# The down projection of a feed-forward layer by quarters, with seven products in place of eight

## The chip, the cores and the metric

The kernel runs on one core of one Trainium2 chip. The metric is the device time of one launch in microseconds (us). The engines are TensorE (PE, with its weight loads as PEld), VectorE (DVE), ScalarE (ACT), GpSimd (POOL) and SyncE (SP), which here only issues DMA transfers. Each engine works through its own instructions in the order in which they were written; semaphores between the engines are set by what reads and writes each buffer.

## The reference

Two transformer blocks on 512 tokens of width 1024, in float32. What the change touches is the end of the second block: a gated feed-forward layer with 2816 inner columns, whose last product is the down projection, and the final norm.

```python
h = rmsnorm_2(x, ffn_norm_g[l])
x = x + (jax.nn.silu(h @ w_gate[l]) * (h @ w_up[l])) @ w_down[l]
...
return rmsnorm_2(x, final_norm_g)
```

Here `w_down` is 2816 x 1024, so the last product is (512 x 2816) @ (2816 x 1024).

## The kernel before

Every float32 product is made of three fast ones: each operand is split into a rounded high part and the rest, and high x high, high x low and low x high are summed in PSUM. An activation block of 128 x 128 is loaded into TensorE as the stationary side, and 512 columns of weights stream past it.

**Weights.** All weights come as one stream of chunks, each 128 x 1024 elements (512 KB: two blocks of 128 rows by 512 columns). For a chunk, SP issues the load into `raw`, a ring of two buffers (`load_to`, L265); ACT copies it to `wh`, the high part (L290); DVE subtracts to get `wl` (L291), which is the last reader of the raw buffer, so that the chunk after the next may be loaded into it. `wh` and `wl` have four buffers each. When TensorE has used chunk i for the last time, `used(i)` calls for the conversion of chunks up to i + 3 and the loading of those up to i + 5. The position of these calls in the program sets the order on SP, ACT and DVE.

**Gate and up.** The two products ahead of the last one are already made with seven products of quarters (class `Sevenfold`): the weights' quarters are loaded (class `Quarters`, tiles `quart`), and DVE adds and subtracts them (L203, tiles `qsum`). The result, the gated activations, stands in three tiles `fa`.

**Down projection.** `dn0` and `dn1` are the two halves of 512 output columns. Each has 22 blocks of 128 inner rows (11 chunks), and every chunk is used by 2 row blocks x 4 token blocks x 3 = 24 matmuls of 512 columns (L378); the two products have 2 x 22 x 4 x 3 = 528 of them. `place` splits the activations from `fa` into `fs` (ACT L480, DVE L481). `ev_dn` adds a finished block to `x5` (DVE L1455), sums the squares (ACT L501), and in the second half makes the norm's factor on POOL (`rstd2`, L493 to L496), scales (ACT L1462, DVE L1463) and sends the block to DRAM.

**Elsewhere.** In the first block's attention POOL normalises the probabilities P (L568, L569), which TensorE then transposes (L607); in the norms POOL makes `var` and `rstd`.

Of the kernel before, what the change touches and what calls it, by code (L numbers as in the profile page):

```python
# [11 lines left out]
F32 = mybir.dt.float32  # L12
FR = mybir.dt.float32r
# [4 lines left out]
S = 512  # L18
# [10 lines left out]
def two_blocks_kernel(  # L29
# [143 lines left out]
    class Quarters:  # L173

        n_loads, n_sums = 0, 0

        def __init__(self, w, c0, n):
            self.w, self.c0, self.half, self.parts = w, c0, n // 2, {}

# [3 lines left out]
        def load(self, name):  # L183
            i, Quarters.n_loads = Quarters.n_loads % 6, Quarters.n_loads + 1
            if i not in ring:
                if i < 4:
                    if 0 not in ring:
                        t = unit("quart", "U3", [128, 4, 1024], F32)
                        ring.update({j: t[:, j, :] for j in range(4)})
                else:  # L190
                    ring[i] = pool.tile([128, 1024], F32, name="quart", tag="raw", bufs=2)
            t = self.parts[name] = self.view(ring[i])
            c, k = self.c0 + self.half * (name[1] == "2"), 512 * (name[2] == "2")
            nc.sync.dma_start(t, self.w[k:k + 512, c:c + self.half].rearrange("(k p) c -> p k c", p=128))
# [19 lines left out]

    specs["fg0"] = ([(w_gate_2, 0, 512, 0)], 8)
    specs_tail = {f"dn{i}": ([(w_down_2, 512 * i, 512, 0)], 22) for i in range(2)}
    quartered = []
    for i in range(6):
        for w in (w_gate_2, w_up_2):
            quartered.append(Quarters(w, 512 * i, 512 if i < 5 else 256))  # L220

# [27 lines left out]
    def load_to(i):  # L249
        while len(raws) <= min(i, len(stream) - 1):  # L250
# [11 lines left out]
            for w, c0, n, at, *heads in pieces:  # L262
                src = w[k0 * 128:(k0 + nk) * 128, c0:c0 + (heads[1] * heads[2] if heads else n)]
                if not heads:
                    nc.sync.dma_start(raw[:, :, at:at + n], src.rearrange("(k p) c -> p k c", p=128))  # L265
                    continue
# [7 lines left out]
    def convert_to(i):  # L274
        while len(ws) <= min(i, len(stream) - 1):
# [13 lines left out]
            for js in [slice(j, min(nk, j + cut)) for j in range(0, nk, cut)]:  # L289
                nc.scalar.copy(hi[:, js], raw[:, js])  # L290
# [13 lines left out]
    side = []  # L304
    mark = [None]
    last_plain = [None]
# [191 lines left out]

    def sum_sq(src, ss, n=512):
        j = p2("junk")  # L500
        nc.scalar.activation(j[:, :n], src, AF.Square, accum_out=ss)  # L501
# [813 lines left out]

    def fa_at(c):
        i = c // 8
        if i not in fa_tiles:
            fa_tiles[i] = unit("fa", ("U5", "U2", "U4")[i], dt=F32)
        return fa_tiles[i], c % 8  # L1320

    class Sevenfold:
# [14 lines left out]
        def out(self, half, t, v):  # L1337

            c, n = half * self.n, self.n
            tok = slice(256 * t, 256 * t + 256)  # L1340
# [7 lines left out]
            else:  # L1348
                ft, at = fa_at(4 * (self.g // 2) + c)
                nc.vector.tensor_mul(ft[:, at:at + n, tok], v, gates[half][:, :n, tok])  # L1350
# [80 lines left out]
    fparts = []  # L1431

    def place(i):
        while len(fparts) <= min(21, i + 3):
            j = len(fparts)
            if j < 20:
                if j % 4 == 0:
                    t = unit("fs", ("U0", "U6", "U1", "U5", "U2")[j // 4])
                    fparts_at[0] = t
                hi, lo = fparts_at[0][:, j % 4, :], fparts_at[0][:, 4 + j % 4, :]  # L1440
            else:
                t = pool.tile([128, 2, 512], FR, name="fs", tag=f"V{j - 20}")
                hi, lo = t[:, 0, :], t[:, 1, :]
            ft, at = fa_at(j)
            split(hi, lo, ft[:, at, :], 0.5)
            fparts.append((hi, lo))
        return fparts[i]

    fparts_at = [None]

    def ev_dn(nh):
        def f(tb, ps):
            c = halves[nh]
            xx = x5[:, tb, c]
            nc.vector.tensor_add(xx, xx, ps)  # L1455
            sum_sq(xx, ssf[:, tb, nh:nh + 1])
            if nh == 0:
                nc.gpsimd.tensor_mul(xx, xx, gfin[:, c])  # L1458
                return
            r = rstd2(ssf[:, tb, :], D)  # L1460
            xa = x5[:, tb, halves[0]]
            nc.scalar.activation(xa, xa, AF.Copy, scale=r)  # L1462
            nc.vector.scalar_tensor_tensor(xx, xx, r, gfin[:, c], op0=OP.mult, op1=OP.mult)  # L1463
            for q in halves if tb == NB - 1 else [slice(0, 1024)]:
                nc.sync.dma_start(ov[:, tb, q], x5[:, tb, q])
        return f

    for nh in range(2):
        run(product(f"dn{nh}", place, ev_dn(nh), True, "mid" if nh == 0 else "tail"))

# [48 lines left out]
```

## Time and profile before

| what | value |
|---|---|
| time, median of 3 runs | 1212.84 us (1212.43 to 1214.42) |
| the profiled execution: its time, its span | 1213.95 us, 1212.2 us |
| PE busy in the span | 1180.9 us (97%) |
| DVE, ACT, POOL busy | 798.0 us (66%), 611.9 us (50%), 234.8 us (19%) |
| share of the 16 DMA engines in use, rate | 30.7%, 97 GB/s |
| the chain that ended last: share of PE | 85% |

The span is the time from the first to the last instruction that the profiler recorded; the launch's own time has 1.75 us around it. The times of the runs are without the profiler. The rows of a trace carry the line of the kernel (L378) and the names of the tiles, output first: `mm<-wh,fs` writes `mm` from `wh` and `fs`. Matmuls are pipelined, so a row's length reaches into the next row: the distance between starts is the cost.

### The profile page before, as it was taken

The page shows a single profiled execution, that of the slowest core. Times are in us where ns is not written, and L with a number is a line of the kernel's source. Part 1 is how long each engine was busy: PE and PEld are TensorE (multiplying, and loading weights), DVE is VectorE, ACT ScalarE, POOL GpSimd, SP SyncE. Part 2 cuts the span into 40 slices and gives each one's busy share as a digit, 9 for nine tenths or more (in the row PEclk, how much of TensorE's full clock was granted, in tenths as well). Part 3 has the DMA queues.
Part 4 walks back from the last instruction along what each step waited for, and adds up shares of the span by engine and source line. Part 5 has one row for each costly group of instructions (what it writes and reads, how often), then busy time and mean ns, then how long its engine had stood idle before and what let it go on. Part 6 is the DMA issues. An engine that isn't in the chain of part 4 may idle for free.

```text
span 1212.2 us, 18380 instructions
## 1 busy us (share of the span) xinstructions
PE 1180.9 (97%) x6700; PEld 1020.6 (84%) x6700; DVE 798.0 (66%) x1526; ACT 611.9 (50%) x1239; POOL 234.8 (19%) x468
## 2 busy tenths in 40 slices
PE   6999999999999999999999999999999999999997
PEld 5898888888888888789888788788899999988885
DVE  5578767796575744785555578773898888793322
ACT  4466456535663444534566667632655544472212
POOL 2011065403341020301433435400000000000201
PEclk9999999999999999999999999999999999999999
DMA  5422302221222532334222221353333342243221
GB/s 192 99 69 70 122 19 70 83 90 44 70 87 88 191 112 92 127 91 115 55 85 83 52 64 53 115 180 107 122 105 119 91 122 79 62 174 122 87 87 70
DMA packets 81946, 117.16 MB, mean 97 GB/s; under 512 B 14528, under 2 KB 44480, under 8 KB 81856
## 3 DMA queue, kind: packets, MB, share of 16 engines
q1 hardware_dynamic: 81856, 115.99, 30.7%
q8 instruction: 53, 0.87, 0.3%
q14 instruction: 37, 0.30, 0.1%
HBM read 109.68 MB, written 6.29 MB: 96 GB/s over the span
## 4 chain that ended last, share of the span: by engine, by line
PE 85%; DVE 5%; issue 3%; ACT 2%; DMA 2%; POOL 1%; SPq 0%; POOLq 0%; DVEq 0%; ACTq 0%
PE mm L378 58%; PE mm L1360 7%; PE R L1360 5%; PE E L1360 5%; PE AV L622 3%; PE T L607 2%; DVE wl L291 2%; DMA raw<-in_w_in_dram 1%; PE T L509 1%; PE S L841 1%; PE S L840 1%; DMA raw<-in_w_branch_b_dram 1%; ACT wh L290 0%; POOL rstd L487 0%; PE S L1189 0%
## 5 line engine op out<-in xcount | busy, mean ns | idle before, releaser
L291 DVE TENSOR_TENSOR wl<-raw,wh 128x512 fp32r<-128x512 f32 (+4 forms) x199 | 183.0, 938 | 146.4 <-ACT wh L290 145.3
L290 ACT CAST wh<-raw 128x512 fp32r<-128x512 f32 (+4 forms) x199 | 155.7, 806 | 195.1 <-PE mm L378 127.0
L378 PE MATMUL mm<-wh,fs 128*128 128x512 f32 x352 | 110.6, 395 | 1.6 <-ACT fs L480 1.6
L568 POOL TENSOR_TENSOR rr<-rs,mone 128x1 f32<-128x1 f32 x128 | 76.4, 597 | 167.4 <-ACT P L562 107.4
L378 PE MATMUL mm<-hh,wh 128*128 128x512 f32 x256 | 103.6, 405 | 0.0
L478 DVE TENSOR_TENSOR pl<-T,ph 128x128 fp32r<-128x128 f32 (+3 forms) x152 | 62.0, 412 | 60.5 <-ACT ph L477 60.0
L378 PE MATMUL mm<-hl,wh 128*128 128x512 f32 x256 | 101.4, 396 | 0.0
L378 PE MATMUL mm<-hh,wl 128*128 128x512 f32 x256 | 100.5, 395 | 0.0
L378 PEld LDWEIGHTS mm<-wh,fs 128*128 128x128 f32 x352 | 65.9, 188 | 18.0 <-ACT fs L480 1.8
L562 ACT ACTIVATE P<-P,nm 128x128 f32<-128x128 f32 (+2 forms) x96 | 51.5, 536 | 51.2 <-DVE nm L555 47.7
L477 ACT CAST ph<-T 128x128 fp32r<-128x128 f32 (+3 forms) x152 | 54.7, 362 | 42.6 <-PE T L607 31.4
L569 POOL TENSOR_SCALAR P<-P,rr 128x256 f32<-128x256 f32 (+3 forms) x128 | 71.8, 561 | 12.0
L290 ACT CAST wh<-qsum 128x1024 fp32r<-128x1024 f32 (+1 forms) x44 | 42.7, 974 | 54.6 <-PE R L1360 23.2
L378 PE MATMUL mm<-wl,fs 128*128 128x512 f32 x176 | 69.7, 397 | 0.3 <-DVE wl L291 0.3
L1458 POOL TENSOR_TENSOR x<-x,gb 128x512 f32<-128x512 f32 x4 | 6.1, 1542 | 283.7 <-ACT junk L501 283.7
L291 DVE TENSOR_TENSOR wl<-qsum,wh 128x1024 fp32r<-128x1024 f32 (+1 forms) x44 | 49.5, 1126 | 13.4 <-ACT wh L290 13.4
L607 PE MATMUL T<-ident,P 128*128 128x128 f32 x296 | 54.6, 278 | 3.7 <-ACT km L1140 2.8
L1360 PE MATMUL R<-acts,wh 128*128 128x256 f32 x320 | 57.8, 281 | 0.0
L1360 PE MATMUL mm<-acts,wh 128*128 128x256 f32 x320 | 57.6, 281 | 0.0
L378 PEld LDWEIGHTS mm<-hh,wl 128*128 128x128 f32 x256 | 48.1, 188 | 11.2
L1360 PE MATMUL E<-acts,wh 128*128 128x256 f32 x320 | 57.1, 281 | 0.0
L378 PEld LDWEIGHTS mm<-hh,wh 128*128 128x128 f32 x256 | 48.2, 188 | 8.6
(410 smaller groups left out, 3338.2 us busy)
## 6 DMA issues: line engine op xcount, KB each, us to landing
raw<-in_w_in_dram SPq DMA_DIRECT2D x50, 512.0 KB, 3.7
raw<-in_w_down_dram SPq DMA_DIRECT2D x22, 512.0 KB, 3.7
quart<-in_w_up_dram SPq DMA_DIRECT2D x20, 512.0 KB, 4.0
raw<-in_w_merge_dram SPq DMA_DIRECT2D x16, 512.0 KB, 3.6
raw<-in_w_out_dram SPq DMA_DIRECT2D x16, 512.0 KB, 4.0
quart<-in_w_gate_dram SPq DMA_DIRECT2D x16, 512.0 KB, 3.9
raw<-in_w_ple_gate_dram SPq DMA_DIRECT2D x8, 512.0 KB, 4.1
raw<-in_w_branch_b_dram SPq DMA_DIRECT2D x4, 512.0 KB, 3.5
```

The costliest lines, as they stand in the source:

```text
L290: nc.scalar.copy(hi[:, js], raw[:, js])
L291: mark[0] = nc.vector.tensor_sub(lo[:, js], raw[:, js], hi[:, js].bitcast(F32)).ins
L378: nc.tensor.matmul(o, x_, m, start=kc == 0 and k == 0 and n0 == 0, stop=last and k == 2)
L477: nc.scalar.copy(hi, src)
L478: nc.vector.tensor_sub(lo, src, hi.bitcast(F32))
L509: nc.tensor.transpose(T[:, i, :], src[:, blk(c + i)], ident)
L562: nc.scalar.activation(P[:, :n], P[:, :n], AF.Exp, bias=bias, scale=-1.0, accum_out=rs)
L568: nc.gpsimd.tensor_tensor(rr, rs, mone, op=OP.pow)
L569: nc.gpsimd.tensor_scalar(P[:, :n], P[:, :n], rr, 1.0, op0=OP.mult, op1=OP.mult)
L607: nc.tensor.transpose(T[:, i, :], P[:, blk(i)], ident)
L622: nc.tensor.matmul(self.av[:, q0:q0 + pc.stop - pc.start], self.v(kb), m, start=pi == 0 and i == 0, stop=pi == len(plan) - 1 and i == 1)
L1360: nc.tensor.matmul(R[:, c, :], w[:, kc, cs], m[:, kc, :], start=first and c + kc + k == 0, stop=kc == 3 and k == 2, skip_group_check=True)
```

## The change

The down projection is made with seven products on quarters in place of eight (`DOWN`). Both operands are cut in two by two: inner rows by 1408, output columns by 512, tokens by 256. Each product has 11 blocks of 128 inner rows and 2 token blocks, so 66 matmuls; seven have 462. The four weight operands that are sums of quarters, S1 to S4, are made in DRAM: 16 transfers of 352 x 512 elements (704 KB) copy quarters into `down_sums` (on SP's queue, behind the loads of chunks 14, 16, ... 44), and 16 transfers of the same size, issued by POOL, add other quarters to them (at chunks 46, 48, ... 76; each behind a one-column copy `poke` from that chunk's `wh`, which fixes its place). The products S1 to S4 then load their chunks from there. A product of 11 blocks has five full chunks and one of half the size, so 42 chunks in place of 22, and a chunk serves 12 matmuls in place of 24.

The activations' sums T1 to T4 are made by DVE in place on `fa` (L1494) and split (ACT L518, DVE L519) in three parts while the product ahead runs. Results that are not accumulated in PSUM are added to `x5` by DVE (L1517). `x5` now comes in eight loads of 256 KB (L1476) in place of four of 512 KB. For the pairing of columns in `fa`, gate and up take their quarters from columns c and c + 1408, and the chunk `fg0` comes in two loads of 256 columns.

```diff
-    specs["fg0"] = ([(w_gate_2, 0, 512, 0)], 8)
-    specs_tail = {f"dn{i}": ([(w_down_2, 512 * i, 512, 0)], 22) for i in range(2)}
+    specs["fg0"] = ([(w_gate_2, 0, 256, 0), (w_gate_2, DFF // 2, 256, 256)], 8)
+    down_sums = {f"S{i}": tc.dram_tile([DFF // 2, 512], F32, name=f"down{i}") for i in range(1, 5)}
+    DOWN = ("A11", "S4", "A12", "S1", "S2", "S3", "A22")
+    specs_tail = {f"dn{name}": ([(down(name), 0, 512, 0)], 11) for name in DOWN}
+    behind, poke = {}, pool.tile([128, 1], F32, name="poke", tag="poke")
+    def plan_sums():
+        copies = [("S1", "A21"), ("S3", "A11"), ("S2", "A11"), ("S4", "A12")]
+        adds = [("S1", "A22"), ("S3", "A21"), ("S2", "S1"), ("S4", "S2")]
+        at = 14
+        for some, engine in ((copies, nc.sync), (adds, nc.gpsimd)):
+            for dst, src in some:
+                for r in range(0, DFF // 2, 352):
+                    behind[at] = (engine, down_sums[dst][r:r + 352, :], down(src)[r:r + 352, :])
+                    at += 2
+    def send(i, hi):
...
+        if engine is nc.sync:
+            with tc.issue_after(loads[0]):
+                engine.dma_start(dst, src)
+        else:
+            with tc.issue_after(engine.tensor_copy(poke, hi[:, 0, 0:1].bitcast(F32)).ins):
+                engine.dma_start(dst, src, accum_op=OP.add, max_dma_last_dim=512)
...
+            send(len(ws), hi)
             ws.append((hi, lo))
...
-    x5 = unit("x5", "U3", [128, NB, 1024], F32)
-    for tb in range(NB):
-        nc.sync.dma_start(x5[:, tb, :], x4v[:, tb, :])
...
-    for nh in range(2):
-        run(product(f"dn{nh}", place, ev_dn(nh), True, "mid" if nh == 0 else "tail"))
+        for b in range(2):
+            nc.sync.dma_start(x5[i, t][b], x4v[:, 2 * t + b, halves[i]])
...
+    def fs_make(name, part):
+        if name in T_OF:
+            d, a, op, b = T_OF[name]
+            nc.vector.tensor_tensor(fa(d, part), fa(a, part), fa(b, part), op=op)
+            src = fa(d, part)
...
+        split(hi, lo, src, 0.5)
...
+    def add_to(i, t, R, op=OP.add):
+        for b in range(2):
+            xx = x5[i, t][b]
+            nc.vector.tensor_tensor(xx, xx, R[b], op=op)
...
+        elif name == "S2":
+            add_to(0, 1, R["U"], OP.subtract)
+            first_done(0, 1)
+            add_to(1, 1, R["U"])
+            add_to(1, 0, R["U"])
...
+        for i, (kc, b) in enumerate(seq):
+            if n < 6 and i in (2, 8, 14):
+                with tc.issue_after(mark[0]), tc.issue_after(mark_hi[0]):
+                    fs_make(DN_ACT[DOWN[n + 1]], i // 6)
+            if n < 4 and i == 10:
+                x_load(*((0, 1), (0, 0), (1, 1), (1, 0))[n])
+            g, j = divmod(kc, 2)
+            convert_to(f0 + g)
...
+            for k, (a, w) in enumerate(((ah, wh), (ah, wl), (al, wh))):
+                nc.tensor.matmul(acc[b], a, w[:, j], start=first and kc == 0 and k == 0, stop=kc == 10 and k == 2,
+                                 skip_group_check=True)
+            if end_of[g] == i:
+                used(f0 + g)
```

Three places of the written order show where instructions now stand. The first is DVE in the down projection, before: the end of the first half `dn0`, with its four additions to `x5`, between the conversions of the chunks.

```order
L291 TENSOR_TENSOR wl_11880<-raw_11814,wh_11879 128x1024
L291 TENSOR_TENSOR wl_11913<-raw_11848,wh_11912 128x1024
L1455 TENSOR_TENSOR x5_11558<-x5_11558,mm_11563 128x512
L1455 TENSOR_TENSOR x5_11558<-x5_11558,mm_11582 128x512
L1455 TENSOR_TENSOR x5_11558<-x5_11558,mm_11589 128x512
L1455 TENSOR_TENSOR x5_11558<-x5_11558,mm_11596 128x512
L291 TENSOR_TENSOR wl_11955<-raw_11883,wh_11954 128x1024
```

DVE after, from the first chunk of product S3 (`wl_12166`) to its third (`wl_12205`); L328 is the same subtraction as L291 above.

```order
L328 TENSOR_TENSOR wl_12166<-raw_12130,wh_12165 128x1024
L1494 TENSOR_TENSOR fa_11214<-fa_11214 128x3x256
L1517 TENSOR_TENSOR x5_11675<-x5_11675,mm_11741 128x512
L1517 TENSOR_TENSOR x5_11910<-x5_11910,mm_11741 128x512
L1517 TENSOR_TENSOR x5_12038<-x5_12038,mm_11741 128x512
L1517 TENSOR_TENSOR x5_11675<-x5_11675,mm_11742 128x512
L1517 TENSOR_TENSOR x5_11911<-x5_11911,mm_11742 128x512
L1517 TENSOR_TENSOR x5_12039<-x5_12039,mm_11742 128x512
L519 SCALAR_TENSOR_TENSOR fs_12117<-fa_10305,fs_12117 128x1024
L328 TENSOR_TENSOR wl_12187<-raw_12148,wh_12186 128x1024
L519 SCALAR_TENSOR_TENSOR fs_12061<-fa_11214,fs_12061 128x768
L328 TENSOR_TENSOR wl_12205<-raw_12169,wh_12204 128x1024
```

Between two subtractions that free the same raw buffer there now stand the last part of the sum, six additions, two splits and the other buffer's subtraction; before, at most four additions and one subtraction.

The second place is SP at the start of the down projection, before.

```order
L265 DMA raw_11449<-in_w_down_2_dram 128x2x512
L265 DMA raw_11470<-in_w_down_2_dram 128x2x512
L103 DMA gb_11556<-in_final_norm_g_2_dram 128x1024
L1429 DMA x5_11558<-x4d_8583 128x1024 x4
L265 DMA raw_11489<-in_w_down_2_dram 128x2x512
L265 DMA raw_11512<-in_w_down_2_dram 128x2x512
L265 DMA raw_11531<-in_w_down_2_dram 128x2x512
```

SP after, the same place.

```order
L302 DMA raw_11506<-in_w_down_2_dram 128x2x512
L302 DMA raw_11527<-in_w_down_2_dram 128x2x512
L103 DMA gb_11613<-in_final_norm_g_2_dram 128x1024
L302 DMA raw_11546<-in_w_down_2_dram 128x2x512
L1476 DMA x5_11675<-x4d_8636 128x512
L302 DMA raw_11569<-in_w_down_2_dram 128x2x512
L1476 DMA x5_11675<-x4d_8636 128x512
L1476 DMA x5_11794<-x4d_8636 128x512 x2
L1476 DMA x5_11910<-x4d_8636 128x512
L1476 DMA x5_11911<-x4d_8636 128x512
L1476 DMA x5_12038<-x4d_8636 128x512
L1476 DMA x5_12039<-x4d_8636 128x512
L302 DMA raw_11588<-in_w_down_2_dram 128x2x512
```

All eight loads of `x5` now stand ahead of the load of the first product's fifth chunk.

The third place is POOL in the norm that begins the second block, before.

```order
L493 TENSOR_SCALAR var<-ssg 128x1
L494 TENSOR_SCALAR var<-ssg,var 128x1
L496 TENSOR_TENSOR rstd<-var,mhalf 128x1
L485 TENSOR_SCALAR var<-ss 128x1
L487 TENSOR_TENSOR rstd<-var,mhalf 128x1
```

POOL after, the same place (the lines of the norm are now L523 to L534).

```order
L531 TENSOR_SCALAR var<-ssg 128x1
L249 COPY poke<-wh 128x1
L250 DMA down_82<-down_80 1408x128
L532 TENSOR_SCALAR var<-ssg,var 128x1
L534 TENSOR_TENSOR rstd<-var,mhalf 128x1
L523 TENSOR_SCALAR var<-ss 128x1
L525 TENSOR_TENSOR rstd<-var,mhalf 128x1
```

An addition for S4 (`down_82`), in 1408 pieces of 128 elements, now stands between the two steps of `var`. The other twelve additions stand in the same way between the POOL instructions of the attention (S1) and of what follows it (S3, S2).

## Rows read from the trace of the kernel before

**Rows 1.** Page: busy time, share of the span, instructions of each engine

```profile
PE 1180.9 (97%) x6700; PEld 1020.6 (84%) x6700; DVE 798.0 (66%) x1526; ACT 611.9 (50%) x1239; POOL 234.8 (19%) x468
```

**Rows 2.** Busy time by stretch: last product, and what follows it

```profile
core 0: us, PE busy (x) PEld busy (x) DVE busy (x) ACT busy (x) POOL busy (x), PEclk, DMA share, GB/s
1077.00:1204.60 127.60, 126.68 (x552) 101.70 (x552) 46.63 (x56) 38.02 (x57) 9.74 (x14) 1.00 0.29 97
1204.60:1212.20 7.60, 0.00 (x0) 0.00 (x0) 1.96 (x3) 2.02 (x4) 1.47 (x3) 0.70 0.46 180
```

**Rows 3.** Groups of instructions by line, 1077 to 1213 us

```profile
L378 PE MATMUL mm<-wh,fs 128*128 128x512 f32 x352 | 110.6, 395 | 1.6 <-ACT fs L480 1.6
L291 DVE TENSOR_TENSOR wl<-raw,wh 128x1024 fp32r<-128x1024 f32 x22 | 28.0, 1273 | 63.0 <-ACT wh L290 63.0
L290 ACT CAST wh<-raw 128x1024 fp32r<-128x1024 f32 x21 | 22.0, 1049 | 67.1 <-PE mm L378 57.2 <-DMA raw<-in_w_down_dram 5.3 <-issue 4.6
L501 ACT ACTIVATE junk<-x 128x512 f32<-128x512 f32 x8 | 5.0, 627 | 17.5 <-DVE x L1455 17.5
L1462 ACT ACTIVATE x<-x,rstd 128x512 f32<-128x512 f32 x4 | 2.9, 724 | 4.4 <-POOL rstd L496 4.4
```

**Rows 4.** Timeline of PE: start, length, instruction, idle time ahead

```profile
1077.57 0.72 PE L378 MATMUL mm<-wh,fs 128*128 128x512 f32 x2 [1.58 <-ACT fs L480]
...
1179.70 0.62 PE L378 MATMUL mm<-wh,fs 128*128 128x512 f32 x2
...
1181.10 0.62 PE L378 MATMUL mm<-wh,fs 128*128 128x512 f32 x2
```

**Rows 5.** DMA issues from 1060 us: count, size, median us to landing

```profile
raw<-in_w_down_dram SPq DMA_DIRECT2D x22, 512.0 KB, 3.7
x<-x4d SPq DMA_DIRECT2D x4, 512.0 KB, 5.5
```

**Rows 6.** Timelines of SP, ACT, DVE: one raw buffer's turn

```profile
1095.65 0.37 SPq L265 DMA_DIRECT2D raw<-in_w_down_dram  x1
...
1099.48 1.05 ACT L290 CAST wh<-raw 128x1024 fp32r<-128x1024 f32 x1 [3.82 <-DMA raw<-in_w_down_dram]
...
1100.56 1.23 DVE L291 TENSOR_TENSOR wl<-raw,wh 128x1024 fp32r<-128x1024 f32 x1 [3.64 <-ACT wh L290]
...
1101.82 0.37 SPq L265 DMA_DIRECT2D raw<-in_w_down_dram  x1
```

**Rows 7.** Timeline of DVE: instructions directly behind one another

```profile
866.12 0.69 DVE L478 TENSOR_TENSOR acts<-h3f,acts 128x512 fp32r<-128x512 f32 x1
866.72 1.22 DVE L203 TENSOR_TENSOR qsum<-qsum,quart 128x1024 f32<-128x1024 f32 x1
867.85 1.22 DVE L203 TENSOR_TENSOR qsum<-quart 128x1024 f32<-128x1024 f32 x1
```

**Rows 8.** Timeline of SP: the issue of two loads

```profile
1066.88 0.88 SPq L265 DMA_DIRECT2D raw<-in_w_down_dram  x2
```

**Rows 9.** Timelines of POOL and PE: a probability block and its transpose

```profile
336.19 0.79 POOL L569 TENSOR_SCALAR P<-P,rr 128x128 f32<-128x128 f32 x1
...
340.27 0.27 PE L607 MATMUL T<-ident,P 128*128 128x128 f32 x1
```

**Rows 10.** Busy time by stretch: where S3's sums are issued

```profile
400.00:420.00 20.00, 20.00 (x92) 16.26 (x91) 12.88 (x19) 6.90 (x12) 0.00 (x0) 1.00 0.70 237
```

**Rows 11.** Timeline of POOL in the norm at 500 us

```profile
503.73 0.86 POOL L494 TENSOR_SCALAR var<-ssg,var 128x1 f32<-128x1 f32 x1 [3.44 <-ACT junk L501]
```

**Rows 12.** Timeline of PE: a pause and the clock behind it

```profile
696.20 0.69 PE L607 MATMUL T<-ident,P 128*128 128x128 f32 x2 [2.79 <-ACT km L1140]
...
697.12 0.63 PE L378 MATMUL mm<-ckl,wh 128*128 128x512 f32 x1
...
699.18 0.40 PE L378 MATMUL mm<-wh,cq 128*128 128x512 f32 x1
```

More of the change, by code (lines that the diff above doesn't have):

```diff
@@ L264, in load_to @@
                 if not heads:
-                    nc.sync.dma_start(raw[:, :, at:at + n], src.rearrange("(k p) c -> p k c", p=128))
+                    loads[0] = nc.sync.dma_start(raw[:, :, at:at + n], src.rearrange("(k p) c -> p k c", p=128)).ins
                     continue
@@ L1314, in two_blocks_kernel, with fa_at @@
     fa_tiles, gates = {}, {}
[L1316 to L1320, printed above, removed]
+    def fa_at(i, half):
+        if i // 2 not in fa_tiles:
+            fa_tiles[i // 2] = unit("fa", ("U5", "U2", "U4")[i // 2], dt=F32)
+        return fa_tiles[i // 2], 4 * half + 2 * (i % 2)
     class Sevenfold:
@@ L1449, in two_blocks_kernel @@
[L1449 to L1466, printed above, removed]
@@ L1468, in two_blocks_kernel, with x_load, fa @@
-    for nh in range(2):
-        run(product(f"dn{nh}", place, ev_dn(nh), True, "mid" if nh == 0 else "tail"))
+    x5 = {}
+    def x_load(i, t):
+        if i == 0:
+            q = pool.tile([128, 2, 512], F32, name="x5", tag=f"V{t}")
+            x5[i, t] = [q[:, 0, :], q[:, 1, :]]
+        else:
+            x5[i, t] = [p2("x5") for _ in range(2)]
+        for b in range(2):
+            nc.sync.dma_start(x5[i, t][b], x4v[:, 2 * t + b, halves[i]])
+    def fa(name, part):
+        f, t = int(name[1]) - 1, int(name[2]) - 1
+        n = 4 if part < 2 else 3
+        return fa_tiles[part][:, 4 * f:4 * f + n, 256 * t:256 * t + 256]
@@ new lines, in two_blocks_kernel, with dn_banks, dn_end @@
+    R = {}
+    def dn_banks(kinds):
+        return [{"mm": mm_bank, "S": s_bank, "AV": av_bank,
+                 "T": lambda: t_bank("E").rearrange("p a b -> p (a b)")}[k]() for k in kinds]
+    def dn_end(name):
+        if name == "A11":
+            R["U"] = dn_banks(("mm", "mm"))
+            for b in range(2):
+                nc.scalar.activation(R["U"][b], R["A11"][b], AF.Copy, scale=-1.0)
+        elif name == "S4":
+            add_to(0, 1, R["S4"])
+        elif name == "A12":
+            add_to(0, 0, R["A11"])
+            first_done(0, 0)
+        elif name == "S1":
+            add_to(0, 1, R["S1"])
+            add_to(1, 1, R["S1"], OP.subtract)
+        elif name == "S2":
[3 more added lines that the diff above has]
+            add_to(1, 0, R["U"])
+        elif name == "S3":
+            add_to(1, 1, R["S3"])
+            for b in range(2):
+                last_done(b, 1)
+            add_to(1, 0, R["S3"])
@@ new lines, in two_blocks_kernel, with dn_product @@
+    DN_ACT = {"A11": "B11", "S4": "B22", "A12": "B21", "S1": "T1", "S2": "T2", "S3": "T3", "A22": "T4"}
+    DN_BANK = {"A11": ("S", "S"), "S4": ("T", "T"), "S1": ("mm", "AV"), "S3": ("T", "T"), "A22": ("S", "S")}
+    def dn_product(n, name):
+        into = {"A12": "A11", "S2": "U"}.get(name, name)
+        if into not in R:
+            R[into] = dn_banks(DN_BANK[name])
+        acc, f0, first = R[into], first_of[f"dn{name}"], into == name
+        seq = [(kc, b) for kc in range(11) for b in range(2)]
+        if n == 6:
+            seq = seq[:16] + [(kc, b) for b in range(2) for kc in range(8, 11)]
+        end_of = {kc // 2: i for i, (kc, b) in enumerate(seq)}
+        for i, (kc, b) in enumerate(seq):
[6 more added lines that the diff above has]
+            convert_to(f0 + g)
+            wh, wl = ws[f0 + g]
+            ah, al = [t[:, kc % 4, blk(b)] for t in fs[DN_ACT[name], kc // 4]]
+            for k, (a, w) in enumerate(((ah, wh), (ah, wl), (al, wh))):
[3 more added lines that the diff above has]
+                used(f0 + g)
+            if n == 6 and kc == 10:
+                xx = x5[1, 0][b]
+                nc.vector.tensor_add(xx, xx, acc[b])
+                last_done(b, 0)
+        dn_end(name)
@@ L1473 @@
+    for part in range(3):
+        fs_make("B11", part)
+    with ordered():
+        for n, name in enumerate(DOWN):
+            dn_product(n, name)
 _INS = ['x', 'p', 'w_in', 'b_forget', 'w_branch_a', 'w_branch_b', 'w_merge', 'w_out', 'g_pre', 'g_post',
```

81 lines of the change are left out of this document (55 added, 26 removed).

## The prediction

> **What bounds the kernel now.** I read the page first: TensorE is busy for 97% of the span, every other engine for two thirds or less [rows 1]. So over the whole kernel, fewer matmuls mean less time, unless something else becomes the slowest in the stage that is changed. So the stage decides, and I read it by itself. From 1077.0 to 1204.6 us TensorE works for 126.68 of 127.60 us, at full clock; after it come 7.6 us without a matmul, the tail [rows 2]. Next come the groups of that stretch [rows 3]: the matmuls wait 1.6 us at the start and hardly again, while ACT's casts wait 57.2 us for TensorE against 5.3 us for a DMA. The reader is to see that today the weights arrive too early, and that TensorE sets the pace. The stage runs from 1077.57 [rows 4] to 1204.6: 127.0 us.
>
> **TensorE's part.** Six matmuls start in 1.40 us (1179.70 to 1181.10), 0.2333 us each [rows 4]. The 528 of before take 123.2 us; the other 24 in the stretch (552 - 528, products of 256 columns that end gate and up) take half as long each, 2.8 us. After, 462 x 0.2333 = 107.8 us: 15.4 us saved, if the weights come in time. A product of 66 takes 15.4 us.
>
> **The loader's part.** A chunk now serves 12 matmuls, 2.8 us, in place of 24, 5.6 us, so weights must come twice as fast. A load takes 3.7 us to land [rows 5]. A raw buffer's turn, when nothing but the buffer holds it up, can be read off: load issued at 1095.65, cast at 1099.48 (1.05 us, after a wait for the DMA), subtraction at 1100.56 (1.23 us), next load issued at 1101.82 [rows 6]: 6.17 us. With the median load and the same steps it is 3.7 + 1.05 + 1.23 and some 0.1 of handover = 6.1 us. Two buffers take turns; of a product's six chunks the first, third and fifth, all full ones, go through one of them, so a product needs three turns: 3 x 6.1 = 18.3 us against TensorE's 15.4. **The loader, not TensorE, sets the pace after the change**, and seven products take 7 x 18.3 = 128.1 us. That alone eats the whole saving of 15.4 us and a little more. The 2.8 us of the old stage's foreign matmuls lie in the first product, as they do now: 130.9.
>
> **What stands between the turns.** DVE works in its written order, and a raw buffer is free only when its subtraction is through. From the end of one subtraction to the cast's end two chunks later a turn leaves DVE 3.7 + 1.05 + 0.1 = 4.85 us. Instructions directly behind one another start 0.60 us apart at 512 columns (866.12 to 866.72) and 1.13 us at 1024 (866.72 to 867.85) [rows 7]; 768 columns lie halfway, 0.87. In that gap after stand a part of a sum (0.87), a split of 1024 (1.13), the other buffer's subtraction (1.13), a split of 768 (0.87) and k additions: 4.00 + 0.60k. That is too long by 0.4 us for k = 2 (in A12 and in S1), 1.6 for k = 4 (in S2 and in A22), 2.8 for k = 6 (in S3, the listing above): 0.4 x 2 + 1.6 x 2 + 2.8 = 6.8. In the last product ACT also has two sums of squares (0.63) and two scalings (0.72) [rows 3] ahead of a cast, 2.7 us of work, the scalings behind POOL's factor; I take 1.2, since part of it lies in the load's time (ends 0 and 2.7). DVE's and ACT's extras: 8.0 us.
>
> **SP.** The eight loads of `x5` stand ahead of the first product's fifth chunk. The issue of a load costs SP 0.44 us (two in 0.88) [rows 8], eight cost 3.5, and their data share the engines with the weights: four loads of twice the size took 5.5 us to land [rows 5]. Walking the written order with these durations, the fifth chunk is 2.3 us later than its buffer allows; ends 0 and 5.5.
>
> **The sum for the stage**: 128.1 + 2.8 + 8.0 + 2.3 = 141.2 us, against 127.0: **+14.2**. The tail stays: behind the last matmul there is the same chain of addition, sum of squares, factor, scaling and transfer (7.6 us, [rows 2]); 0 to 0.7 more, taken at 0.
>
> **The sums in the background.** The copies move 704 KB each, 16 of them, on SP, while the DMA engines are little used (about 100 GB/s in the stage [rows 2]); chunks are loaded ahead, so I take 0, with ends 0 and 2. The additions cost POOL its issue, which no row shows. The lower bound is the issue of a load on SP, 0.44 us [rows 8]; the upper is that figure by pieces, 1408 here against the 256 (128 partitions x 2 rows) of a weight load: 0.44 x 5.5 = 2.4 us. At S1's four additions POOL has a block of P ready at 336.98 (336.19 + 0.79) that TensorE transposes at 340.27 [rows 9]: 3.3 us cover it. At S3's POOL stands idle, 0.00 of 20 us [rows 10], and so it nearly is at S2's. S4's four stand in the norm, between two steps of `var`; POOL waited there 3.44 us for a sum of squares [rows 11], so an issue may lie in that wait, or delay `rstd` and with it TensorE. I take 0.3 us for each of these four, an eighth of the upper bound, since the wait is longer than the issue: 1.2 us, with ends 0 (all of it in the wait) and 4 x 2.4 = 9.6 (none). If the cover is gone, each addition costs its whole issue.
>
> **From the sum to the time.** 14.2 + 1.2 = 15.4. The profiled execution took 1213.95 us (span 1212.2 and 1.75 around it); 1213.95 + 15.4 = 1229.35. It was 1.1 above the median of the runs, 1212.84, so the median comes to 1228.2, as a round figure **1228**. What measurement can tell from no change is 0.2%, 2.4 us.
>
> **Rivals.**
> (a) *TensorE stays the bound* and the change gives what its count says: 107.8 + 2.8 = 110.6 us, -16.4, 1196.4. It decides where a turn falls to 15.4 / 3 = 5.1 us, that is a load lands in 2.8 us. For it: today's loads are 512 KB while the engines run at under a third [rows 2], and a load that meets no other may be quicker than the median. Against: the turn of [rows 6] shows 3.8 us. Chance 0.09.
> (b) *The ring alone*: DVE's extras and the `x5` loads vanish in slack that the four `wh`/`wl` buffers give: 130.9 us, +3.9, about 1217. For it: a late subtraction need not stop TensorE at once. Against: every turn follows the last, so lateness adds up. Chance 0.15.
> (c) *The clock falls too.* After a pause of 2.79 us (ending at 696.20) the matmuls from 697.12 to 699.18 start 0.41 us apart (five of them), after 699.18 0.23 again [rows 12]: 1.2 in place of 2.4 GHz for some 3 us, which cost about 1.3 us. Pauses of that length could come in S2, S3 and A22, where DVE's gap is longest; two in each and the time is 6 x 1.3 = 8 us longer: 1236. The Trainium skill ("TensorE: Matmul & The Clock Gate", section "HAM oscillation — how this bites in real kernels") tells of a kernel whose matmuls wait for each weight slice and restart at the lower clock every time; by it the cost would come back with each pause, and this trace shows one such pause but no series of them. Against: most pauses I expect are under 2.8 us. Chance 0.09.
> (d) *POOL is the slow one.* An addition's issue takes twice my upper bound, 4.8 us. Then each of S1's four exceeds the cover by 1.5 and delays the transposes (6 us), and S4's four stand in the norm's chain, each costing up to 3 (12 us): +18 at worst, half of it likely, 1237 to 1246. The Trainium skill ("SBUF — State Buffer", section "SBUF: two separate sides") says that transfers issued by GpSimd have their descriptors made by GpSimd's own cores, and that some DVE instructions lock them out meanwhile; no row of this trace shows such a transfer, so that stays a reason for the rival alone. Chance 0.12.
> (e) *Nothing to measure*, within 2.4 us of 1212.8: the loader's loss and TensorE's gain meet by chance, at a turn of 5.8 us with few extras. Chance 0.04.
> The forecast itself, 1222 to 1233, has 0.51.
>
> **How the numbers follow.** The time is the likeliest case's. To hold 8 in 10 the range takes in that case, (b), (c) and the nearer half of (d), together 0.81, and the upper half of (e), 0.02 more: 1212 to 1245. The likeliest one's own range, 1222 to 1233, comes from the ends of the `x5` loads, of ACT's share and of POOL. Faster: (a) and a little of (b), 0.11; same: (e) and the lowest of (b), 0.05; slower: the rest, 0.84.
>
> **What the profile after would show.** In the last 141 us TensorE at work for 110.6 us, near 78%, waiting for `wl` and `wh`; ACT's casts waiting for the DMA of `raw`, not for TensorE; a load issued right behind each subtraction and landing 3.7 us later; the longest stalls where additions stand, in S2's, S3's and A22's products. On POOL the additions' issues, under 2.4 us each, and the stretch to 1077 us no longer than before by more than 2 us. The prediction is wrong if the casts still wait for TensorE, if loads land in under 3 us, or if the time is added ahead of the last product.

## The result and the profile after

The changed kernel takes **1243.7 us** (median of 4 runs, 1242.7 to 1247.74) against 1213.16 for the kernel before on the same chip (4 runs): a ratio of 1.0257 with a 95% interval of 1.0232 to 1.0282, or +30.5 us where +15.2 was forecast. Its profiled execution is the longest of the four, 1247.74 us with a span of 1246.0. The span grew by 33.8 us: 8.2 us ahead of the down projection, whose first matmul starts at 1085.74 in place of 1077.57 [rows 4], 26.0 us in that stage (153.0 for 127.0), and -0.4 in the tail (7.25 for 7.6 [rows 2]).

The page after, its busy times [rows 1] and GpSimd's own DMA queue (packets, MB, share of the 16 engines' time):

```profile
PE 1184.7 (95%) x6634; PEld 1015.1 (81%) x6634; DVE 848.4 (68%) x1569; ACT 637.4 (51%) x1260; POOL 274.2 (22%) x500
q0 software_dynamic: 22784, 11.54, 7.8%
```

TensorE has 66 matmuls fewer and is busy longer. That alone doesn't show a lower clock: in product A12 below, at a granted clock of 1.00, 66 matmuls are recorded as busy for 16.39 us in place of 15.4, since a row's length reaches past the next row's start. The clock is read from PEclk. The new queue q0 carries the additions: 11.54 MB in 22784 packets, some 500 bytes each.

Busy time by stretch after, one row for each of the seven products (A11, S4, A12, S1, S2, S3, A22) and one for the tail; columns as in [rows 2]:

```profile
core 0: us, PE busy (x) PEld busy (x) DVE busy (x) ACT busy (x) POOL busy (x), PEclk, DMA share, GB/s
1085.74:1108.95 23.21, 20.76 (x91) 16.59 (x91) 12.03 (x16) 8.70 (x11) 0.00 (x0) 0.93 0.63 215
1108.95:1128.12 19.17, 16.72 (x67) 12.16 (x67) 9.87 (x10) 9.31 (x12) 0.00 (x0) 1.00 0.44 152
1128.12:1146.26 18.14, 16.39 (x66) 12.00 (x66) 12.10 (x13) 7.45 (x9) 0.00 (x0) 1.00 0.47 154
1146.26:1168.66 22.40, 17.04 (x67) 12.02 (x67) 16.19 (x15) 9.75 (x14) 3.77 (x2) 1.00 0.42 122
1168.66:1189.46 20.80, 17.58 (x66) 13.55 (x67) 16.05 (x17) 9.46 (x10) 0.00 (x0) 0.92 0.49 152
1189.46:1212.77 23.31, 18.50 (x68) 14.32 (x66) 17.80 (x20) 9.74 (x14) 2.73 (x3) 0.85 0.39 124
1212.77:1238.75 25.98, 19.89 (x67) 13.85 (x65) 12.97 (x16) 9.44 (x15) 5.07 (x9) 0.87 0.36 112
1238.75:1246.00 7.25, 0.00 (x1) 0.00 (x0) 2.10 (x3) 1.69 (x4) 0.81 (x2) 0.67 0.38 145
```

No product reaches 15.4 us; A12, with the least beside it, takes 18.1, close to the 18.3 of three turns of a buffer. No engine is full in any row. What they wait for is in the groups by line of the same stage, and in the list of TensorE's waits (total us, times, longest):

```profile
L328 DVE TENSOR_TENSOR wl<-raw,wh 128x1024 fp32r<-128x1024 f32 (+1 forms) x42 | 49.5, 1185 | 46.9 <-ACT wh L327 46.8
L327 ACT CAST wh<-raw 128x1024 fp32r<-128x1024 f32 (+1 forms) x42 | 40.6, 974 | 80.3 <-DMA raw<-down 46.2 <-DMA raw<-in_w_down_dram 34.0
...
PE mm L1588 <- DVE wl L328: 7.1, 5, 2.5
PE E L1588 <- DVE wl L328: 6.3, 3, 4.8
PE S L1588 <- ACT wh L327: 5.2, 5, 1.8
```

In [rows 3] the casts waited 57.2 us for TensorE and 5.3 for the DMA. Now all of their 80 us is for the DMA, and TensorE waits for DVE's subtractions and ACT's casts: the chain has turned round.

What is lost ahead of the stage is not spread. Matched matmul by matmul, the trace after runs 0.7 us behind that of before at 480 us, 8.4 at 520, 10.3 at 575 and 8.9 at 1075. I call this last figure the drift. (The stage starts 8.2 us later and not 8.9, since TensorE waits 0.9 us ahead of its first matmul in place of the 1.6 of [rows 3].) It arises where the last additions stand. GpSimd's queue and the DMA issues (count, size, us to landing) from 470 to 535 us:

```profile
q0 software_dynamic: 5696, 2.88, 37.6%
raw<-in_w_in_dram SPq DMA_DIRECT2D x6, 512.0 KB, 7.5
down<-down POOLq DMA_DIRECT2D x4, 704.0 KB, 13.3
```

A weight load that takes 3.7 us here without additions (next section) takes 7.5 beside additions that take 13.3. Timelines of SP, ACT and PE show the slowest one of this stretch:

```profile
478.26 0.37 SPq L302 DMA_DIRECT2D raw<-in_w_ple_gate_dram  x1
...
487.77 1.04 ACT L327 CAST wh<-raw 128x1024 fp32r<-128x1024 f32 x1 [4.38 <-DMA raw<-in_w_ple_gate_dram]
...
488.86 0.50 PE L416 MATMUL mm<-wh,x2h 128*128 128x512 f32 x1 [2.71 <-ACT wh L327]
```

Issued at 478.26, cast at 487.77: 9.5 us, and TensorE stands still for 2.71 us behind it. A late load also reaches TensorE by way of the norm, since ACT works in order (ACT and PE):

```profile
517.72 1.05 ACT L327 CAST wh<-raw 128x1024 fp32r<-128x1024 f32 x1 [2.76 <-DMA raw<-in_w_in_dram]
...
520.35 0.63 ACT L539 ACTIVATE junk<-eb 128x512 f32<-128x512 f32 x1
...
527.82 1.94 PE L547 MATMUL T<-ident,xn 128*128 128x128 f32 x8 [2.54 <-DVE xn L555]
```

The norm's sum of squares (L539) stands behind a cast that waited 2.76 us for its load, and TensorE waits 2.54 us for what that norm makes.

### The profile page after: what moved, and what is told of

Read it like the earlier page. It is cut to its first block, busy times and chain, and to the rows that moved or that the text cites. A ratio compares the mean times of both kernels' runs of the same rounds, so it can differ in the third digit from the quotient of the medians.

```text
span 1246.0 us, 18470 instructions
## 1 busy us (share of the span) xinstructions
PE 1184.7 (95%) x6634; PEld 1015.1 (81%) x6634; DVE 848.4 (68%) x1569; ACT 637.4 (51%) x1260; POOL 274.2 (22%) x500
## 3 DMA queue, kind: packets, MB, share of 16 engines
q0 software_dynamic: 22784, 11.54, 7.8%
## 4 chain that ended last, share of the span: by engine, by line
PE 68%; DMA 10%; DVE 9%; issue 5%; ACT 4%; POOL 3%; SPq 0%; POOLq 0%; ACTq 0%; DVEq 0%
PE mm L416 43%; PE mm L1398 7%; PE R L1398 5%; PE E L1398 4%; DVE wl L328 4%; DMA raw<-down 3%; DMA raw<-in_w_down_dram 3%; ACT wh L327 3%; PE AV L660 2%; PE T L645 2%; DMA raw<-in_w_in_dram 2%; PE T L547 1%; DMA raw<-in_w_ple_gate_dram 1%; DMA raw<-in_w_branch_b_dram 1%; PE S L879 1%
## 5 line engine op out<-in xcount | busy, mean ns | idle before, releaser
L328 DVE TENSOR_TENSOR wl<-raw,wh 128x512 fp32r<-128x512 f32 (+4 forms) x219 | 204.0, 949 | 133.8 <-ACT wh L327 133.3
L327 ACT CAST wh<-raw 128x512 fp32r<-128x512 f32 (+4 forms) x219 | 173.3, 814 | 215.4 <-PE mm L416 63.8
L327 ACT CAST wh<-qsum 128x1024 fp32r<-128x1024 f32 (+1 forms) x44 | 42.8, 974 | 54.6 <-PE R L1398 23.2
L328 DVE TENSOR_TENSOR wl<-qsum,wh 128x1024 fp32r<-128x1024 f32 (+1 forms) x44 | 49.5, 1126 | 13.4 <-ACT wh L327 13.4
L416 PEld LDWEIGHTS mm<-hl,wh 128*128 128x128 f32 x256 | 48.3, 189 | 7.8
L416 PE MATMUL mm<-h2h,wh 128*128 128x512 f32 x128 | 53.7, 419 | 0.0
L327 ACT CAST wh<-quart 128x1024 fp32r<-128x1024 f32 (+1 forms) x33 | 32.1, 973 | 37.0 <-PE mm L1398 19.5
```

The lines of the kernel that those rows point to most:

```text
L327: mark_hi[0] = nc.scalar.copy(hi[:, js], raw[:, js]).ins
L416: nc.tensor.matmul(o, x_, m, start=kc == 0 and k == 0 and n0 == 0, stop=last and k == 2)
```

## The experiments

Stage is the time from the first matmul of the down projection to the end of its last, drift as above, both from each run's profile. Ratios are to the kernel before on the same chip, with 95% intervals. Five of the kernels have the same additions at the same places (after, four and three raw buffers, no gain, outputs late); their drifts, 5.0 to 10.6 us, show how far it moves from one execution to another.

| run | ratio (interval) | drift, us | stage, us |
|---|---|---|---|
| after | 1.0257 (1.0232 to 1.0282) | 8.9 | 153.0 |
| no additions | 1.0190 (1.0172 to 1.0207) | 0.4 | 150.7 |
| plain copies in their place | 1.0199 (1.0176 to 1.0221) | 1.4 | 150.6 |
| POOL's time only | 1.0161 (1.0146 to 1.0177) | 2.2 | 145.5 |
| last additions moved | 1.0205 (1.0175 to 1.0235) | 3.5 | 149.7 |
| plain transfers by GpSimd | 1.0196 (1.0176 to 1.0217) | 2.4 | 150.1 |
| additions in 2 KB pieces | 1.0216 (1.0196 to 1.0236) | 5.1 | 150.3 |
| four raw buffers | 0.9947 (0.9929 to 0.9965) | 5.0 | 114.4 |
| three raw buffers | 0.9951 (0.9937 to 0.9966) | 8.0 | 116.1 |
| no gain on GpSimd | 1.0209 (1.0192 to 1.0226) | 5.8 | 147.8 |
| outputs late | 1.0225 (1.0210 to 1.0240) | 10.6 | 146.7 |
| four changes together | 0.9881 (0.9866 to 0.9896) | 0.7 | 111.7 |

### What the additions cost, and by what

**No additions.**

```diff
-        for some, engine in ((copies, nc.sync), (adds, nc.gpsimd)):
+        for some, engine in ((copies, nc.sync),):
```

> Leaves out the sixteen additions (and their one-column copies on POOL); S1 to S4 then hold single quarters. Landmarks of the two traces put +8.9 us ahead of the down projection, all between 480 and 570 us, where the last additions stand. Theory 1 (the additions' transfers, in flight, make the weight loads late) and theory 2 (POOL's issue delays the norms, the forecast's mechanism) both expect the time after, 1243.7, less 8.9: 1235 us. If the copies carry part of the cost, it stays above 1237.

Measured 1238.04 us; drift 0.4. DMA issues of this run from 470 to 535 us:

```profile
raw<-in_w_in_dram SPq DMA_DIRECT2D x6, 512.0 KB, 3.7
```

The drift is gone with the additions and the loads land in 3.7 us again; the sixteen copies cost nothing that shows, as forecast. The time is 3 us above what was expected; on this chip the kernel before took 1215.5 us too, 2.3 more than in the pair with the changed kernel.

**Plain copies in their place, on SP.**

```diff
-        for some, engine in ((copies, nc.sync), (adds, nc.gpsimd)):
+        for some, engine in ((copies, nc.sync), (adds, nc.sync)):
```

> The sixteen additions become plain copies of the same bytes at the same chunks, on SP's queue, with nothing on POOL; the sums are not made. Theory 1 in the form that the bytes count: the weight loads behind them land as late as after, 1242 to 1245 us. Theory 1 in the form that the additions' way of moving counts (512-byte pieces, read and written back): loads 1 to 3 us late only, 1235 to 1239. Theory 2 (POOL): 1235, no cost left.

Measured 1238.04 us; drift 1.4. From 470 to 535 us:

```profile
raw<-in_w_in_dram SPq DMA_DIRECT2D x6, 512.0 KB, 4.8
down<-down SPq DMA_DIRECT2D x4, 704.0 KB, 6.9
```

The same bytes at the same chunks make the loads 1.1 us later, and most of that lies in slack. So the bytes alone don't make the 8.9.

**POOL's time without a transfer.**

```diff
-            with tc.issue_after(engine.tensor_copy(poke, hi[:, 0, 0:1].bitcast(F32)).ins):
-                engine.dma_start(dst, src, accum_op=OP.add, max_dma_last_dim=512)
+            engine.tensor_copy(poke, hi[:, 0, 0:1].bitcast(F32))
+            engine.tensor_tensor(poke, poke, poke, op=OP.mult)
+            for _ in range(3):
+                engine.tensor_tensor(poke, poke, mhalf, op=OP.pow)
```

> Keeps POOL busy for about 1.9 us at the sixteen places (a square and three powers on one column) in place of issuing a transfer; the sums are not made. Theory 2 (POOL's time between the norm's steps): about 1243, as after. Theory 1 (transfers in flight): 1235 to 1236, as without additions.

Measured 1234.24 us; drift 2.2. GpSimd was held for 3.0 to 8.6 us at the sixteen places (median 3.8), longer than the 1.9 that was meant and than an addition's issue. Even so the drift is only 1.8 us above that without additions (one execution each), and not the 8.9. This run's stage is the shortest of those on two buffers without a change to it, mainly because the written order of its last product came out otherwise; "Outputs late" comes back to it.

**The last additions moved.**

```diff
                     at += 2
+                    at += 33 if at == 68 else 0
```

> S4's four additions move from chunks 70, 72, 74, 76 to 103, 105, 107, 109, whose weights are ready 14 to 28 us before their first use in the trace of before (against 1 to 4 us at 70 to 76). Theory 1: the cost falls to what the addition at chunk 68 leaves, 0 to 2 us: 1235 to 1237. Theory 2: also gone from the norm, but POOL then stands in the second block's attention, where it scales probabilities: 1235 to 1240. A rival that the additions cost the same anywhere (4 x 2 us): 1243.

Measured 1239.59 us; drift 3.5. The edit moved five additions, S2's last and S4's four, to chunks 101 to 109, and two of them (at 101 and 105) were never issued, since these chunks take another path through the conversion; so S2 and S4 are incomplete, and this is a run of 14 additions. It shows the drift down from 8.9, not a clean price; the run with four changes, below, moves all five.

**Plain transfers, issued by GpSimd at the same places.**

```diff
-                engine.dma_start(dst, src, accum_op=OP.add, max_dma_last_dim=512)
+                engine.dma_start(dst, src, max_dma_last_dim=512)
```

> The sixteen additions become plain transfers of the same pieces (128 elements), still issued by GpSimd at the same places; the sums are not made. If the small pieces make the loads late, the drift ahead of the down projection stays at 6 to 9 us, 1241 to 1244 us. If it is the reading and writing back of the addition, the drift falls to 1 to 3 us, 1235 to 1239.

Measured 1239.56 us; drift 2.4. The issue took 1.23 and 0.94 us (medians of two sets of eight) where an addition's took 2.17 and 1.53, and a transfer landed after 6.7 us (median) where an addition took 12.5. From 470 to 535 us:

```profile
q0 software_dynamic: 768, 2.88, 13.1%
down<-down POOLq DMA_DIRECT2D x5, 704.0 KB, 5.6
raw<-in_w_in_dram SPq DMA_DIRECT2D x6, 512.0 KB, 5.6
```

The pieces did not stay small: GpSimd's queue moved 2.88 MB in 768 packets, some 3750 bytes each. So the run shows that GpSimd's issuing is not the cost, but doesn't part the pieces from the addition.

**Additions in larger pieces.**

```diff
-                engine.dma_start(dst, src, accum_op=OP.add, max_dma_last_dim=512)
+                engine.dma_start(dst, src, accum_op=OP.add, max_dma_last_dim=2048)
```

> The sixteen additions stay, in pieces of 512 elements (2 KB) in place of 128. If the count of pieces is what makes the loads late, an addition lands in 6 to 8 us in place of 12.5, GpSimd's issue falls below 1 us, and the drift ahead of the down projection falls to 1 to 4 us: 1235 to 1239 us. If the addition itself does, it stays at 6 to 9 us: 1241 to 1244. What the sums hold in this form is not relied on.

Measured 1241.55 us; drift 5.1. From 470 to 535 us:

```profile
q0 software_dynamic: 1472, 2.88, 25.9%
raw<-in_w_in_dram SPq DMA_DIRECT2D x6, 512.0 KB, 6.8
down<-down POOLq DMA_DIRECT2D x4, 704.0 KB, 7.5
```

GpSimd's issue fell to 0.98 us and an addition landed in 8.5 us (median of sixteen, 7.1 to 11.4) in place of 12.5 (10.8 to 15.9), and still the loads beside it take 6.8 us where a plain transfer leaves them at 4.8 (from SP) or 5.6 (from GpSimd). For the same 2.88 MB the packets take 37.6% of the 16 DMA engines' time with additions in 512-byte pieces, 25.9% in 2 KB pieces, and 13.1% as plain transfers in 3750-byte pieces. So the adding most likely costs by itself; no run has additions and plain transfers in pieces of one size. How much the pieces add is not settled. The drift of 5.1 lies inside the 5.0 to 10.6 that the small pieces gave; but counted from 480 us on alone, where the last additions stand, it grows by 2.3 us here and by 4.7 to 10.0 in the five runs with small pieces (1.0 without additions), which speaks for the pieces, in one execution.

### What sets the pace of the stage

**Four raw buffers**, two more from the second product on, in space that is free by then.

```diff
-            raw = pool.tile([128, 1024], F32, name="raw", tag="raw", bufs=2)
+            m = len(raws) - first_of["dnA11"]
+            if m >= 6 and m % 4 > 1:
+                if m % 4 not in more:
+                    more[m % 4] = pool.tile([128, 1024], F32, name="raw", tag="idx") if m % 4 == 2 else q4("raw")
+                raw = more[m % 4]
+            else:
+                raw = pool.tile([128, 1024], F32, name="raw", tag="raw", bufs=2)
```

> From the second product on, the weights' chunks go through four raw buffers in place of two; nothing else changes. Theory 1 (the turn of two buffers sets the pace of the down projection): the stage, 153 us in the profile after, falls to between 115 and 128 us, since TensorE needs 15.4 us and VectorE at most some 16 us for a product: 1206 to 1219 us. Rival: VectorE's order and the fallen clock set the pace, with the loads waiting for them: stage of 142 us or more, 1232 us or more.

Measured 1208.24 us. Busy time by stretch in this run, products S1 and S3:

```profile
1134.53:1149.86 15.33, 15.33 (x68) 12.39 (x66) 15.33 (x14) 9.97 (x13) 4.48 (x2) 1.00 0.62 187
...
1165.26:1180.66 15.40, 15.40 (x67) 12.45 (x66) 15.40 (x18) 9.25 (x13) 12.68 (x3) 1.00 0.60 191
```

Every product from the second on takes 15.2 to 15.5 us, TensorE's own 66 x 0.2333, at full clock. The work on all engines and the additions are the same, and the stage is 38.6 us shorter. The written order is not quite the same: with more buffers the subtractions stand among DVE's additions (in S3 one stands between the third and the fourth), and the last loads stand ahead of the outputs on SP. A12 shows the buffers by themselves. In the trace after, each of its loads is issued 0.03 us behind a subtraction, and of its five full chunks all but the second are cast 0.1 us behind the landing and subtracted 0.03 us behind the cast, so only the turn holds them up: 18.1 us, and 15.2 here. In S1 and S3 DVE is busy for the whole stretch as well, so there is no more to be had there from the loads.

**Three raw buffers.**

```diff
-            if m >= 6 and m % 4 > 1:
+            if m >= 6 and m % 3 == 2:
...
-                raw = more[m % 4]
+                raw = more[2]
```

> As after, with three raw buffers in place of two from the second product on. Theory 1 by its numbers: a turn of 6.1 us over three buffers is 2.0 us for a chunk, less than TensorE's 2.8, so even with VectorE's extras of up to 2.8 us in a product TensorE sets the pace: products of 15.4 to 17 us, stage 114 to 124 us, 1206 to 1216 us. Rival (four buffers helped by letting loads run far ahead, not by the turn): products of 17 us or more, 1218 us or more.

Measured 1210.1 us, stage 116.1, the second product 16.5 and those behind it 15.2 to 15.5. One more buffer does nearly all of it, as a turn of 6.1 us over three buffers says (2.0 us a chunk against 2.8).

**No gain on GpSimd**: the first 512 output columns are not multiplied by the final gain.

```diff
-            nc.gpsimd.tensor_mul(xx, xx, gfin[:, halves[i]])
```

In the trace after, timelines of POOL and DVE in product S1; a subtraction and a split of these sizes take 1.23 and 0.95 us elsewhere:

```profile
1150.26 3.77 POOL L1523 TENSOR_TENSOR x<-x,gb 128x512 f32<-128x512 f32 x2 [283.62 <-ACT att L539]
...
1150.59 2.29 DVE L328 TENSOR_TENSOR wl<-raw,wh 128x1024 fp32r<-128x1024 f32 x1
1152.80 2.04 DVE L519 SCALAR_TENSOR_TENSOR fs<-fa,fs 128x768 fp32r<-128x768 f32 x1
```

> Leaves out GpSimd's four multiplications of the first 512 output columns by the final gain. In the trace after, subtractions and splits on VectorE beside these four take 2.29 and 2.04 us in place of 1.23 and 0.95. Theory (GpSimd's instruction holds VectorE's up): the products S1 and S3 become 2.2 and 1.1 us shorter, and the time 3 us: 1240 to 1241, with no subtraction of a chunk over 1.3 us. Rival (the long ones lie in slack): within 1 us of after.

Measured 1239.77 us. S1 takes 19.6 us in place of 22.4, S3 21.6 in place of 23.3, and of the 219 subtractions none takes over 1227 ns (the third figure of the lengths), where after the longest took 2294:

```profile
L328 DVE TENSOR_TENSOR wl<-raw,wh x219: 279/958/1227, 10.2 to 1224.9; 128x512 fp32r<-128x512 f32 x54, 128x1024 fp32r<-128x1024 f32 x48, 128x128 fp32r<-128x128 f32 x4, 128x768 fp32r<-128x768 f32 x2
```

GpSimd's multiplications hold DVE's instructions up, by 1.1 us each, and with two buffers that reaches TensorE: 2.8 + 1.7 = 4.5 us between these two executions. Against the medians of the eight two-buffer runs that have the multiplications (S1 22.0, S3 23.0) it is 2.3 + 1.4 = 3.7.

**Outputs late.** SP after, in the last product (timeline), and the subtraction on DVE that frees the buffer for its fifth chunk:

```profile
1219.16 1.22 DVE L328 TENSOR_TENSOR wl<-raw,wh 128x1024 fp32r<-128x1024 f32 x1
...
1221.85 2.20 SPq L1531 DMA_DIRECT2D out_dram<-x  x2
1224.15 0.39 SPq L302 DMA_DIRECT2D raw<-in_w_down_dram  x1
```

The buffer is free at 1220.38. The load is issued at 1224.15, 3.8 us later, since two outputs, which wait for ACT's scaling, stand ahead of it on SP.

```diff
-        nc.sync.dma_start(ov[:, tb, halves[0]], xa)
+        outs.append((ov[:, tb, halves[0]], xa))
...
-        nc.sync.dma_start(ov[:, tb, halves[1]], xx)
+        outs.append((ov[:, tb, halves[1]], xx))
+        if t == 0:
+            send_outs()
...
+    def send_outs():
+        with tc.issue_after(loads[0]):
+            while outs:
+                nc.sync.dma_start(*outs.pop(0))
```

> The four output transfers of the second token half are issued behind the last weight load in place of ahead of the last two. Theory (SP waits for the scaling before it issues the last product's fifth chunk, and its load then shares the engines with the outputs): the last product, 26.0 us, falls to 21 to 23 us, 1239 to 1241 us. Rival (its length comes from the clock alone): 25 us or more, 1243 us.

Measured 1242.1 us. The last product takes 21.3 us in place of 26.0, and the fifth chunk's load is issued 0.03 us behind its subtraction. The run with GpSimd's time alone shows the same without this edit: there the four outputs are out of the way early (DVE and SP),

```profile
1211.86 1.22 DVE L330 TENSOR_TENSOR wl<-raw,wh 128x1024 fp32r<-128x1024 f32 x1
...
1213.10 2.76 SPq L304 DMA_DIRECT2D raw<-in_w_down_dram  x2
```

and its last product takes 20.5 us. In the seven two-buffer runs in which the load is 3.8 us late, the last product takes 23.0 to 26.0 us (median 24.5); the two of them whose clock stays at 1.00 in it take 23.0 and 23.2. So the wait on SP is worth some 2 us by itself, and the 4.7 between these two executions hold a fallen clock as well (PEclk 0.87 against 1.00). The time fell by less than 4.7, and this run's drift was 10.6.

**Four changes together**: four buffers, outputs late, the loads of `x5` each behind the weight load of their place, and the last five additions at chunks 110 to 118.

```diff
-        at = 14
+        places = iter([*range(14, 68, 2), 110, 112, 114, 116, 118])
...
-                    behind[at] = (engine, down_sums[dst][r:r + 352, :], down(src)[r:r + 352, :])
-                    at += 2
+                    behind[next(places)] = (engine, down_sums[dst][r:r + 352, :], down(src)[r:r + 352, :])
...
-                x_load(*((0, 1), (0, 0), (1, 1), (1, 0))[n])
+                with tc.issue_after(loads[0]):
+                    x_load(*((0, 1), (0, 0), (1, 1), (1, 0))[n])
```

> Four raw buffers, the outputs behind the last load, each pair of loads of x5 behind the weight load of its place, and the last five additions moved to chunks 110 to 118, whose weights are ready 8 to 24 us early. If the ring, the additions' transfers and SP's order are what made the change slower, the stage is 113 to 120 us and nothing is lost ahead of it: 1200 to 1207 us, faster than both kernels. If not, it stays above the time before, 1213.

Measured **1200.1 us**, a ratio of 0.9881 (0.9866 to 0.9896): 1.2% faster than the kernel before, and faster than the changed one. The first two products in this run:

```profile
1077.53:1096.79 19.26, 18.54 (x91) 15.33 (x92) 15.05 (x18) 11.41 (x14) 0.00 (x0) 1.00 0.62 196
1096.79:1112.19 15.40, 15.40 (x68) 12.37 (x66) 10.73 (x11) 9.29 (x11) 0.00 (x0) 1.00 0.78 262
```

Stage 111.7, within 1.1 of the 110.6 that TensorE needs; drift 0.7, with all sixteen additions made. Eleven of them stand where they stood; the last five, moved to where the weights are ready early, cost next to nothing there.

## Why the forecast was right in its direction and half its size

**Right: the loader sets the pace.** Three turns of 6.1 us make 18.3 us for a product; A12 took 18.1 (18.7 with its extra on DVE). A11 took 23.2 against 23.4, but that is partly luck: in the run with four changes, where most loads of `x5` come later, it takes 19.3 and not the 21.1 that the forecast leaves without them. So those loads seem to cost more than the 2.3 taken (the fifth chunk's took 6.7 us to land), and the turns less, with two chunks loaded ahead of the stage. The loads landed in 3.6 to 3.8 us (medians of the full chunks), the casts waited for the DMA alone, and a third buffer gives 37 of 38.6 us back. Rival (a), TensorE as the bound, is what the kernel becomes with that buffer.

**Right: copies and tail.** The copies left no drift (0.7 us at 480 us), and the tail was 7.25 for 7.6.

**Wrong: the price of the sums in the background.** The step "the additions cost POOL its issue", taken at 1.2 us, priced the wrong resource. The issue was well bounded (2.17 and 1.53 us between 0.44 and 2.4), and with GpSimd held for longer than that the drift is 2.2. But an addition is in flight for 10.8 to 15.9 us, and a weight load beside it lands after 7.5 us in place of 3.7. At chunks 70 to 76 the weights were only 1 to 4 us early, so TensorE waited; at 490 and 528 us the clock fell to 1.2 GHz for 3.4 us each, behind pauses of 2.71 and 2.54, much as at [rows 12]. From 490.63 to 493.62 us the matmuls start 0.43 us apart in place of 0.23, which makes some 1.4 us of the loss (an estimate). Measured: 8.9 us, 5.0 to 10.6 over the five runs. The forecast's bounds for this term looked at one engine's queue and not at the loads that share the DMA engines.

**Wrong: the stage, +14.2 forecast, +26.0 measured.** The step that failed is "Walking the written order": it was made for the `x5` loads and not for the outputs, although they are DMAs that the change moves on the same queue; and GpSimd's multiplications by the final gain stand in no term. Of the 11.8 us between forecast and measurement the first took up to 4.7 and the second 4.5 in this execution; over the runs, by medians, they are 3.6 and 3.7, the first with the fallen clock that goes with it. (This execution is also the longest of the six two-buffer runs whose stage has the same written order: 149.7 to 153.0 us, median 150.5.) The forecast took 1.23 us for a subtraction from a single row [rows 6]; the mean of 22, 1273 ns [rows 3], held one of 2.29 us already, beside just such a multiplication, and there it lay in slack:

```profile
1144.17 2.29 DVE L291 TENSOR_TENSOR wl<-raw,wh 128x1024 fp32r<-128x1024 f32 x1 [0.44 <-ACT wh L290]
```

A size was off as well: ACT's share in the last product, taken at 1.2 us, is 2.4 to 2.9 in eight of the nine two-buffer runs, the time from the fourth chunk's landing to its cast, which stands behind two scalings. The last 2.6 us, spread over the products in which the forecast had 18.3 to 21.1, are not settled.

**Open: the clock.** Rival (c) came in part: in the stage after the granted clock was 1.2 GHz for 20.5 us in all (at 1088, 1176, 1197 and 1231 us), which the rows show as PEclk 0.85 to 0.93. Here a slower TensorE partly spends time that it would have waited, so the rows don't give its cost, and no run took the clock alone away. One pair ahead of the stage shows a price: TensorE pauses for 2.63 us before 512.94 in the kernel before and for 2.61 before 512.35 without additions, and only in the second does the clock fall behind it, to 1.2 GHz for 3.4 us. From there to 520 us the second run loses 1.3 us on the first, the forecast's price for one fall; and a pause of that length doesn't always bring one. With three or four buffers the clock stays at 1.00 from the second product on.

## What to carry to other kernels

When a change makes fewer matmuls out of each weight chunk, work out the turn of one raw buffer (load, cast, subtraction) and divide it by the number of buffers: if that exceeds TensorE's time on a chunk, the loader eats the saving. Here 6.1 us over two buffers stood against 2.8, and one more buffer brought the saving back. Price a background transfer by what its flight does to the loads beside it, and put it where the weights are ready well ahead of use; and where a queue is walked, walk every transfer on it, outputs too. A group's mean that is above its usual row is a row to look for.

## What the runs showed of the hardware

An adding transfer of 704 KB within DRAM took 12.5 us to land (median of sixteen) where plain ones, from SP or GpSimd, took 6 to 7. It doubled the time of the weight loads beside it (7.5 us for 3.7), which plain ones of the same bytes lengthened by 1.1 us (from SP) and 1.9 (from GpSimd).

GpSimd and VectorE hold each other up. VectorE's subtraction took 2.29 us in place of 1.23 beside one of GpSimd's multiplications. The other way round it is worse: in the run with four buffers VectorE is busy for the whole of S3 (15.40 of 15.40 us, last row of that fence), and there the same multiplication of 512 columns took 1.89 us once and 11.46 us the next time (1.88 and 11.42 in the run with four changes), as the timeline of POOL in that run shows:

```profile
1167.25 1.89 POOL L1529 TENSOR_TENSOR x<-x,gb 128x512 f32<-128x512 f32 x1 [26.25 <-ACT att L545]
1169.21 0.19 POOL L537 TENSOR_SCALAR var<-ssf 128x1 f32<-128x1 f32 x1
1170.06 11.46 POOL L1529 TENSOR_TENSOR x<-x,gb 128x512 f32<-128x512 f32 x1 [0.65 <-ACT att L545]
```

VectorE's own instructions beside it kept their usual lengths (1.21 us for a subtraction of 1024 columns). That VectorE's work is what lengthens GpSimd's is read from these rows; no run took that work away.
